# The first chunks of the first feed-forward layer: both token blocks multiplied before their norm factor is known

## The chip, the cores and the metric

The kernel runs on one core of one Trainium2 chip. The metric is the device time of one execution in microseconds (us), and lower is better. The median of three runs of the kernel before is 754.53 us (754.26 to 755.93).

## What is computed

The reference is one decoder layer in float32 over 256 tokens of width 1024: a half feed-forward layer, a mixing layer with two branches (a state-space branch and differential attention), and a second half feed-forward layer, each between two RMS norms. Only the start matters here, the first feed-forward layer (`x @ w` is a matrix product, `g` a gain per channel):

```python
def rmsnorm(x, g):
    y = x * lax.rsqrt(jnp.mean(x * x, axis=-1, keepdims=True) + EPS)
    return y * g

def swiglu(x, w_gate, w_up, w_down):          # 1024 -> 2816 -> 1024
    return (jax.nn.silu(x @ w_gate) * (x @ w_up)) @ w_down

h = x
h = h + 0.5 * rmsnorm(swiglu(rmsnorm(h, ffn1_pre_g), ffn1_w_gate, ffn1_w_up, ffn1_w_down), ffn1_post_g)
...
```

The norm's factor is one number per token. It can be taken out of a product: `(r * u) @ w` equals `r * (u @ w)`, if `r` is applied to the rows of the result. Both kernels use that, for one token block or for two.

## The kernel before

**Split numbers.** Every operand of the large products is split into a high part that TensorE takes exactly and a low part, the rest; a product is the sum of three: high x high, low x high, high x low. For weights, ScalarE casts the raw chunk to `whi` (L167) and VectorE subtracts to get `wlo` (L168). For activations, ScalarE makes the high part (L343) and VectorE the low part (L345) out of the transposed block in PSUM, each with the gain of the channel.

**Tiles.** The 256 tokens are two blocks of 128, b = 0 and 1. The 1024 channels are two halves, q = 0 and 1, of four k-tiles each. Weights come through three raw buffers of 1 MB; a buffer is loaded again when VectorE has subtracted its last part. The first four chunks are the first 512 columns of the gate weights (chunks 0 and 1, for the two halves of the channels) and of the up weights (chunks 2 and 3). Chunk 0 is loaded and split by single k-tiles, chunks 1 to 3 in two parts. Each chunk needs 4 k-tiles x 3 terms x 2 blocks = 24 matmuls of 128 x 512, 96 in all. From chunk 4 on, the kernel goes another way (`mm_w`, L206: weights stationary, both blocks at once; its first tiles are `pg_f` and `pup_f`).

**Order.** At the start the order on TensorE, ScalarE, VectorE and the DMA queue of SyncE (SP) is the program's own (`own_order`), until `free_order` behind the first four chunks. GpSimd (POOL) runs in program order too. SP loads x in four pieces of 256 KB (b0 q0, b0 q1, b1 q0, b1 q1; L274), and then the chunks (L147).

**The first norm.** ScalarE squares and sums block 0 (`sq_f`, L325), VectorE block 1 (L364), GpSimd makes the factors `r_f` (L330, L331). `turn` (L336) is the step from a block's half to its split, transposed form: four transposes on TensorE into `pu_f` (L340), then L343 and L345. Block 0 is turned without its factor, into `raw_u`; its factor is applied when its products are evicted (`settle`). Block 1 is scaled first by GpSimd (`un_f`, L373), and then turned into the tile `u_f` that the later chunks read. Block 0's part of `u_f` comes later: GpSimd puts the factors on a diagonal (`dr_f`, L378), TensorE multiplies it with ones (`rb_f`, L385), so that every partition has all factors, ScalarE copies that (`rbs_f`, L387), VectorE multiplies the transposed block with gain and factors (`us_f`, L392), and the result is split (L191, L192).

**The products.** `Norm.products` goes over (block, gate or up) in the order (0, gate), (1, gate), (0, up), (1, up), with two chunks each. Gate results are evicted through SiLU (`sg_f`, L245), up results multiplied in (L529, L531), and `back` (L537) transposes the result of a block for the down product.

**Warm-up.** `warm(WARM)` and `warm(FILL)` are matmuls of the identity that nobody reads: 6 ahead of the gain's transpose (`pt_cols_f`, L299), 8 ahead of the first product. Each is two passes of 128 columns.

Of the kernel before, what the change touches and what calls it, by code (L numbers as in the profile page):

```python
# [24 lines left out]
P = 128  # L25
# [12 lines left out]
AHEAD = 3  # L38
WARM = 6
FILL = 8  # L40
TAIL = 3
# [7 lines left out]
def tile_hybrid_layer(ctx: ExitStack, tc: tile.TileContext, x, ffn1_pre_g, ffn1_w_gate, ffn1_w_up,  # L49
# [33 lines left out]
    def bg(shape, name):  # L83
        return ps.tile(shape, F32, tag="bg", name=name, bufs=5)
# [65 lines left out]
    def split_steps(ahead=True):  # L150


        i = len(splits)
        load_to(i + 1)
        r, shape = raws[i], chunks[i][1]
        nj = shape[1] // 2
        his, los = [], []
        splits.append((his, los))
        for q in range(2):
            hi = k4([P, nj, shape[2]], f"whi{i}{q}", F32R)  # L160
            lo = k4([P, nj, shape[2]], f"wlo{i}{q}", F32R)
            his.append(hi)
            los.append(lo)
            n = 1 if i == 0 else nj
            for j in range(0, nj, n):
                js = slice(j, j + n)
                nc.scalar.copy(hi[:, js, :], r[:, q * nj + j:q * nj + j + n, :])  # L167
                nc.vector.tensor_sub(lo[:, js, :], r[:, q * nj + j:q * nj + j + n, :], hi[:, js, :].bitcast(F32))  # L168
                yield
        raws[i] = None  # L170
        if ahead:
            load_to(i + 1 + RAW_BUFS)
# [49 lines left out]
    def mm_nat(acc, w, act, k0, first, last, late):  # L222
# [7 lines left out]
        for i, ((a, b), j) in enumerate(terms):  # L230
            nc.tensor.matmul(acc, a(k0 + j), b(j), start=first and i == 0, stop=last and i == 11)  # L231


    act_since, act_fence = [], [None]
# [53 lines left out]

    pw = bg([P, P], "warm")

# [6 lines left out]
    cols_f = const.tile([P, KD], F32, name="cols_f")  # L297
    pt = bg([P, KD], "pt_cols_f")
    nc.tensor.transpose(pt, stage_f, ident[:KD, :KD])  # L299
# [35 lines left out]
    last_pool = [None]  # L335
    def turn(b, q, src, g, to, name):  # L336

        pu = bg([P, 4, P], f"pu_{name}{b}{q}")
        for i in range(4):
            nc.tensor.transpose(pu[:, i, :], src[:, i * P:(i + 1) * P], ident)  # L340
        hi, lo = to(q)
        for i in range(4):
            nc.scalar.activation(hi[:, i, :], pu[:, i, :], AF.Identity, scale=g(q * 4 + i))  # L343
        for i in range(4):
            nc.vector.scalar_tensor_tensor(lo[:, i, :], pu[:, i, :], g(q * 4 + i), hi[:, i, :].bitcast(F32),  # L345
                                           ALU.mult, ALU.subtract)
        return pu

# [8 lines left out]

    def rms(b, tag, eng=None):

        ss = tiny(2, f"ss_{tag}{b}")  # L360
        for q in range(2):
            src = h[:, b, halves[q]]
            if eng is nc.vector:
                nc.vector.scalar_tensor_tensor(jk([P, 512], f"sq_{tag}{b}{q}"), src, 1.0 / D, src, ALU.mult,  # L364
                                               ALU.mult, accum_out=ss[:, q:q + 1])
            else:
                sum_sq(ss[:, q:q + 1], src, 1.0, f"sq_{tag}{b}{q}")
        return rstd_of(ss, 1.0, f"r_{tag}{b}")
# [11 lines left out]

    def rescaled(pus, r, g, tag, dr):

        dr = diag(r, tag) if dr is None else dr
        rb = bg([P, P], f"rb_{tag}")
        nc.tensor.matmul(rb, ones, dr, start=True, stop=True)  # L385
        rbs = k2([P, P], f"rbs_{tag}")
        nc.scalar.copy(rbs, rb)  # L387
        out = []
        for q in range(2):
# [6 lines left out]

    def set_u(us):
        for q in range(2):
            split(*in_u(0)(q), us[q])

# [57 lines left out]
    class Norm:  # L458
# [3 lines left out]
        def __init__(self, tag, g):  # L462
            self.tag, self.g, self.pus = tag, g, []
            new_u(tag)
            self.to0 = in_u(0)
            self.dr = None
            self.left = []
# [8 lines left out]

        def unit1(self, engs=(nc.vector, nc.vector)):
            r = rms(1, self.tag)
            self.un = [unit(1, q, r, self.tag, engs[q]) for q in range(2)]

        def turn1(self, q):
            turn(1, q, self.un[q], self.g, in_u(1), self.tag)

        def products(self, ws, evict, at, turns=((0, 0), (0, 1), (1, 0), (1, 1)), late="u"):

            n = 0
            for b, i in turns:
                act = of_block(self.to0 if b == 0 else in_u(1))  # L490
                acc = pj(f"pn_{self.tag}{b}{i}")
                for c in range(2):
                    mm_nat(acc, ws[2 * i + c], act, c * 4, c == 0, c == 1, late if b == 0 else "u")
                    n += 1
                    for f in at.get(n, ()):
                        f()
                if b == 1:
                    evict(b, i, acc, None)
                else:
                    self.left.append(lambda i=i, acc=acc: evict(0, i, acc, self.r0))  # L500
            free_order()
# [11 lines left out]
        def rescale(self):  # L513
            set_u(rescaled(self.pus, self.r0, self.g, self.tag, self.dr))

    def ffn(post_v, tag, norm, ready, turned, then, at, ws=None, **kw):
        gu = []
# [22 lines left out]
        norm.products(ws or [take(1) for _ in range(4)], evict,  # L540
                      {n: [f if f else lambda: back(0) for f in fs] for n, fs in at.items()}, **kw)
        back(1)
# [36 lines left out]
    warm(FILL)  # L579
    load_to(1 + RAW_BUFS)  # L580

    def gains():
# [10 lines left out]
    def next_norm(tag, name):  # L593
# [68 lines left out]
    norm.products([take(1) for _ in range(4)], evict_v,  # L662
                  {3: [norm.turns1], 5: [norm.settle, norm.rescale]})

# [483 lines left out]
    ffn(ffn2_post_g, "f2", norm, store, lambda: None, lambda: None,  # L1148
        {3: [norm.turns1], 5: [norm.settle, norm.rescale], 7: [None]})

# [33 lines left out]
```

## Time and profile before

| what | value |
|---|---|
| median of three runs | 754.53 us (754.26 to 755.93) |
| the profiled execution | 753.31 us, of which 751.60 is the span of the core |
| TensorE busy | 742.0 us of the span |
| VectorE, ScalarE, GpSimd busy | 522.1, 437.9, 41.0 us |
| TensorE's granted clock over the span | 0.999 |
| TensorE busy in the first 35 us | 32.80 us |

PE is TensorE's matmuls, PEld its weight loads, DVE VectorE, ACT ScalarE, POOL GpSimd, and SPq the DMA issues of SyncE. A row of the timeline has the start and the duration in us, the engine, the line of the kernel, the operation, the tile written and the tiles read, the shape, the count of merged instructions, and in brackets the idle time in front and what ended it. The duration of a merged row runs from its first start to its last end. A matmul's duration is longer than its distance to the next, because they are pipelined.

### The profile page before, as it was taken

What the parts mean: (1) busy time and instruction counts of PE and PEld (TensorE: products, weight loads), DVE (VectorE), ACT (ScalarE), POOL (GpSimd) and SP (SyncE); (2) the same over time, 40 slices, a digit from 0 to 9 for tenths busy, and PEclk for the clock granted to TensorE, in tenths of its full rate; (3) what the DMA queues carried; (4) which work ended last, traced back from release to release, by engine and by line L of the source; (5) the groups of instructions that cost most, each with busy time, mean ns of one, the idle gap of its engine ahead of it and who ended that gap; (6) DMA issues with size and microseconds to landing.
All of it is one profiled execution on the core that took longest, in us unless ns stands there. A gap on an engine that the chain in (4) does not pass through costs nothing.

```text
span 751.6 us, 11066 instructions
## 1 busy us (share of the span) xinstructions
PE 742.0 (99%) x4385; PEld 643.8 (86%) x4385; DVE 522.1 (69%) x790; ACT 437.9 (58%) x731; POOL 41.0 (5%) x76
## 2 busy tenths in 40 slices
PE   8999999999999999999999999999999999999996
PEld 7888888888889999898999778788888888888885
DVE  6685667654577888868777987696684867766612
ACT  7475556643565565858867555783563756664511
POOL 7400000000200000000000000000010000000000
PEclk9999999999999999999999999999999999999999
DMA  8685666486253647565556454376371777544701
GB/s 316 158 276 162 222 224 240 181 280 223 64 168 115 203 135 242 169 200 183 161 168 202 166 192 152 129 230 246 112 232 49 225 223 224 177 176 184 275 1 56
DMA packets 94212, 137.96 MB, mean 184 GB/s; under 512 B 2684, under 2 KB 68304, under 8 KB 94160
## 3 DMA queue, kind: packets, MB, share of 16 engines
q1 hardware_dynamic: 91488, 129.51, 52.3%
q0 software_dynamic: 2368, 7.22, 3.2%
q8 instruction: 34, 0.56, 0.3%
q10 hardware_dynamic: 304, 0.53, 0.2%
q14 instruction: 18, 0.15, 0.1%
HBM read 136.17 MB, written 1.08 MB: 183 GB/s over the span
## 4 chain that ended last, share of the span: by engine, by line
PE 96%; DVE 1%; POOL 1%; DMA 1%; ACT 1%; issue 0%; SPq 0%; DVEq 0%; POOLq 0%; ACTq 0%
PE acc_f L433 16%; PE pup_f L216 9%; PE pg_f L216 9%; PE pws L231 6%; PE pgt L231 6%; PE pn_f L231 5%; PE pg_f L215 4%; PE pup_f L215 4%; PE acc_mx L433 3%; PE pn_mx L231 3%; PE pwd L231 3%; PE pxs L204 2%; PE pxs L202 2%; PE pxs L201 2%; PE pz L204 2%; PE pz L201 2%
## 5 line engine op out<-in xcount | busy, mean ns | idle before, releaser
L168 DVE TENSOR_TENSOR wlo<-raw,whi 128x1024 fp32r<-128x1024 f32 (+1 forms) x246 | 291.6, 1213 | 53.6 <-ACT whi L167 50.9
L167 ACT CAST whi<-raw 128x1024 fp32r<-128x1024 f32 (+1 forms) x246 | 247.3, 1044 | 56.7 <-PE acc_f L433 22.7
L216 PE MATMUL pg_f<-u_f,whi 128*128 128x512 f32 x288 | 101.2, 396 | 0.0
L216 PE MATMUL pup_f<-u_f,whi 128*128 128x512 f32 x288 | 101.1, 396 | 0.0
L215 PE MATMUL pg_f<-u_f,wlo 128*128 128x256 f32 x252 | 70.5, 280 | 0.0
L215 PE MATMUL pup_f<-u_f,wlo 128*128 128x256 f32 x252 | 70.3, 279 | 0.0
L216 PEld LDWEIGHTS pg_f<-u_f,whi 128*128 128x128 f32 x288 | 52.9, 188 | 9.8
L216 PEld LDWEIGHTS pup_f<-u_f,whi 128*128 128x128 f32 x288 | 52.7, 188 | 9.8
L433 PE MATMUL acc_f<-whi,gh_f 128*128 128x512 f32 x176 | 58.2, 390 | 0.0
L433 PE MATMUL acc_f<-wlo,gh_f 128*128 128x512 f32 x176 | 58.1, 389 | 0.0
L433 PE MATMUL acc_f<-whi,gl_f 128*128 128x512 f32 x176 | 58.1, 389 | 0.0
L215 PEld LDWEIGHTS pg_f<-u_f,wlo 128*128 128x128 f32 x252 | 47.5, 188 | 1.7
L215 PEld LDWEIGHTS pup_f<-u_f,wlo 128*128 128x128 f32 x252 | 47.5, 189 | 1.6
L220 DVE TENSOR_TENSOR su_f<-pup_f,su_f 128x256 f32<-128x256 f32 x36 | 15.2, 422 | 40.5 <-ACT su_f L219 40.5
L433 PEld LDWEIGHTS acc_f<-wlo,gh_f 128*128 128x128 f32 x176 | 33.0, 188 | 6.9
L433 PEld LDWEIGHTS acc_f<-whi,gl_f 128*128 128x128 f32 x176 | 33.0, 188 | 6.8
L433 PEld LDWEIGHTS acc_f<-whi,gh_f 128*128 128x128 f32 x176 | 33.0, 188 | 6.8
L231 PE MATMUL pgt<-whi,u_mx 128*128 128x512 f32 x128 | 34.8, 400 | 0.0
L201 PE MATMUL pz<-u_mx,whi 128*128 128x256 f32 x128 | 32.3, 288 | 0.0
L219 ACT COPY su_f<-pup_f 128x256 f32<-128x256 f32 x36 | 13.4, 371 | 32.2 <-PE pup_f L216 32.1
L202 PE MATMUL pz<-u_mx,whi 128*128 128x256 f32 x128 | 31.8, 284 | 0.0
L201 PE MATMUL pxs<-u_mx,whi 128*128 128x256 f32 x128 | 31.7, 285 | 0.0
(310 smaller groups left out, 1435.9 us busy)
## 6 DMA issues: line engine op xcount, KB each, us to landing
raw<-in_w_in_dram SPq DMA_DIRECT2D x40, 1024.0 KB, 5.4
raw<-in_ffn_w_down_dram SPq DMA_DIRECT2D x22, 1024.0 KB, 5.0
raw<-in_ffn_w_gate_dram SPq DMA_DIRECT2D x20, 1024.0 KB, 5.7
raw<-in_ffn_w_up_dram SPq DMA_DIRECT2D x20, 1024.0 KB, 5.5
raw<-in_ssd_w_branch_dram SPq DMA_DIRECT2D x8, 1024.0 KB, 5.1
acb<-acd POOLq DMA_DIRECT2D x8, 512.0 KB, 4.9
raw<-in_da_w_branch_dram SPq DMA_DIRECT2D x4, 1024.0 KB, 5.1
raw<-in_w_out_dram SPq DMA_DIRECT2D x4, 1024.0 KB, 5.0
```

Source lines behind the costliest of these rows:

```text
L167: nc.scalar.copy(hi[:, js, :], r[:, q * nj + j:q * nj + j + n, :])
L168: nc.vector.tensor_sub(lo[:, js, :], r[:, q * nj + j:q * nj + j + n, :], hi[:, js, :].bitcast(F32))
L201: nc.tensor.matmul(acc[m], wh(j)[:, cs], ah(k0 + j), start=first and j == ks[0], stop=False)
L202: nc.tensor.matmul(acc[m], wh(j)[:, cs], al(k0 + j), start=False, stop=False)
L204: nc.tensor.matmul(acc[m], wl(j)[:, cs], ah(k0 + j), start=False, stop=last and j == ks[-1])
L215: nc.tensor.matmul(acc[:, :T], wl(j)[:, cs], ah(j), start=False, stop=False)
L216: nc.tensor.matmul(acc, wh(j)[:, cs], ahl(j), start=j == 0, stop=j == KD - 1)
L219: nc.scalar.copy(dst[:, m, :], acc[:, T:])
L220: nc.vector.tensor_tensor(dst[:, m, :], acc[:, :T], dst[:, m, :], ALU.add)
L231: nc.tensor.matmul(acc, a(k0 + j), b(j), start=first and i == 0, stop=last and i == 11)
L433: nc.tensor.matmul(acc[b][q], x_[:, ts], w_(kt)[:, halves[q]], start=i == 0 and kt == 0 and x_ is ah and w_ is wh, stop=i == n - 1 and kt ...
```

## The change

Both blocks are now turned without their factor, and all four chunks are multiplied with these raw blocks. `mm_both` takes a chunk k-tile by k-tile and, within it, block by block; two accumulators are open at once. The transposes of the second halves stand inside chunk 0's products (behind 14 and 18 of 24 terms), the second block's `rb` inside chunk 1's (behind 16 terms). The factors come into both blocks' results at eviction, and into both parts of `u_f` by way of `rb`, `rbs`, `us` and the split, once for each block. GpSimd no longer scales block 1, and makes two diagonals.

SP loads the first halves of x (both blocks), then chunk 0, then the second halves, then the other chunks. VectorE casts the first k-tile of chunk 0 in ScalarE's place. VectorE squares block 0 and ScalarE block 1. `WARM` is 5 in place of 6, `FILL` 2 in place of 8. The second norms further on keep their way of working; their functions are only cut up differently.

```diff
-WARM = 6
-FILL = 8
+WARM = 5
+FILL = 2
...
-                nc.scalar.copy(hi[:, js, :], r[:, q * nj + j:q * nj + j + n, :])
+                copy = nc.scalar.copy if i + q + j else nc.vector.tensor_copy
+                copy(hi[:, js, :], r[:, q * nj + j:q * nj + j + n, :])
+                if not i + q + j:
+                    yield
                 nc.vector.tensor_sub(lo[:, js, :], r[:, q * nj + j:q * nj + j + n, :], hi[:, js, :].bitcast(F32))
...
+    def mm_both(accs, w, acts, k0, first, last, between={}):
+        wh, wl = w
+        his = [[(b, a, wh, j) for b in range(2) for a in acts[b]] for j in range(4)]
+        los = [[(b, acts[b][0], wl, j) for b in range(2)] for j in range(4)]
+        terms = his[0] + his[1] + los[0] + his[2] + los[1] + his[3] + los[2] + los[3]
+        for i, (b, x_, w_, j) in enumerate(terms):
+            nc.tensor.matmul(accs[b], x_(k0 + j), w_(j), start=first and j == 0 and w_ is wh and x_ is acts[b][0],
+                             stop=last and j == 3 and w_ is wl)
+            if i + 1 in between:
+                between[i + 1]()
...
-    for b in range(2):
-        for q in range(2):
+    for q in range(2):
+        for b in range(2):
             nc.sync.dma_start(h[:, b, halves[q]], xv[:, b, halves[q]])
-    load_to(RAW_BUFS)
+        load_to((1, RAW_BUFS)[q])
...
-    norm = Norm("f1", lambda j: cols_f[:, j:j + 1])
-    raw_u = [k4([P, 4, 2, P], f"raw_u{q}", F32R) for q in range(2)]
-    norm.to0 = lambda q: (raw_u[q][:, :, 0, :], raw_u[q][:, :, 1, :])
-    norm.r0 = rms(0, "f1")
-    r1 = rms(1, "f1", nc.vector)
-    norm.un = [unit(1, q, r1, "f1", nc.gpsimd) for q in range(2)]
-    norm.dr = diag(norm.r0, "f1")
-    norm.turn0(0)
-    for _ in split_steps(False):
-        pass
-    norm.turn0(1)
-    warm(FILL)
-    load_to(1 + RAW_BUFS)
...
+    def raised(b, q):
+        pus[b][q] = transposed(b, q, h[:, b, halves[q]], "f1")
+
+    def raw(b, q):
+        gained(pus[b][q], q, gain_f, *raw_to[b](q))
+
+    square(ss_f[0], 0, 0, "f1", nc.vector)
+    raised(0, 0)
+    raised(1, 0)
+    warm(FILL)
+    steps = split_steps(False)
+    next(steps)
+    raw(0, 0)
+    raw(1, 0)
+    for _ in steps:
+        pass
+    load_to(1 + RAW_BUFS)
+
+    def first_products(evict, back):
+        acts = [of_block(to) for to in raw_to]
+        acc = [[pj(f"pn_f1{b}0") for b in range(2)], None]
+        mm_both(acc[0], take(1), acts, 0, True, False, {14: lambda: raised(0, 1), 18: lambda: raised(1, 1)})
+        square(ss_f[0], 0, 1, "f1", nc.vector)
+        r = [rstd_of(ss_f[0], 1.0, "r_f10")]
+        dr = diag(r[0], "f10")
+        raw(0, 1)
+        raw(1, 1)
+        rb = bg([P, 2, P], "rb_f1")
+        rbs = []
+        w = take(1)
+        rbs.append(on_rows(rb[:, 0, :], dr, "f10"))
+        for q in range(2):
+            square(ss_f[1], 1, q, "f1")
+        r.append(rstd_of(ss_f[1], 1.0, "r_f11"))
+        us = rescaled(pus[0], rbs[0], gain_f, "f10")
+        dr = diag(r[1], "f11")
+        w2 = take(1)
+        mm_both(acc[0], w, acts, 4, False, True, {16: lambda: rbs.append(on_rows(rb[:, 1, :], dr, "f11"))})
+        set_u(0, us)
+        acc[1] = [pj("pn_f101"), bg([P, 512], "pn_f111")]
+        for b in range(2):
+            evict(b, 0, acc[0][b], r[b])
+        us = rescaled(pus[1], rbs[1], gain_f, "f11")
+        mm_both(acc[1], w2, acts, 0, True, False)
+        w = take(1)
+        set_u(1, us)
+        mm_both(acc[1], w, acts, 4, False, True)
+        split_to(5)
+        for b in range(2):
+            evict(b, 1, acc[1][b], r[b])
+        free_order()
+        back(0)
...
-    ws = [take(1) for _ in range(2)]
-    more = lambda: ws.append(take(1))
     made, ready, turned = next_norm("mx", "mx")
-    ffn(ffn1_post_g, "f1", norm, ready, turned, gains,
-        {1: [norm.turns1], 2: [more], 4: [norm.settle, more], 5: [norm.rescale], 7: [norm.settle, None]}, ws,
-        turns=((0, 0), (1, 0), (0, 1), (1, 1)), late="w")
+    ffn(ffn1_post_g, "f1", ready, turned, gains, first_products)
```

`transposed` and `gained` are the two halves of `turn`; `square` is one half of `rms`; `on_rows` is the matmul and copy that `rescaled` began with. `raw_to[b]` gives block b's raw tiles, `gain_f` the gain columns.

More of the change, by code (lines that the diff above doesn't have):

```diff
@@ L387, in rescaled @@
         nc.scalar.copy(rbs, rb)
+        return rbs
+    def rescaled(pus, rbs, g, tag):
         out = []
@@ L475, in turn0, with unit1, products @@
             self.pus.append(turn(0, q, h[:, 0, halves[q]], self.g, self.to0, self.tag))
[L477 removed]
+        def unit1(self):
             r = rms(1, self.tag)
[L479 removed]
+            self.un = [unit(1, q, r, self.tag, nc.vector) for q in range(2)]
         def turn1(self, q):
             turn(1, q, self.un[q], self.g, in_u(1), self.tag)
[L484 removed]
+        def products(self, evict, at):
+            ws = [take(1) for _ in range(4)]
             n = 0
[L489 removed]
+            for b in range(2):
                 act = of_block(self.to0 if b == 0 else in_u(1))
[L491 to L500, printed above, removed]
+                for i in range(2):
+                    acc = pj(f"pn_{self.tag}{b}{i}")
+                    for c in range(2):
+                        mm_nat(acc, ws[2 * i + c], act, c * 4, c == 0, c == 1, "u")
+                        n += 1
+                        for f in at.get(n, ()):
+                            f()
+                    if b == 1:
+                        evict(b, i, acc, None)
+                    else:
+                        self.left.append(lambda i=i, acc=acc: evict(0, i, acc, self.r0))
             free_order()
@@ L513, in rescale, with ffn @@
         def rescale(self):
-            set_u(rescaled(self.pus, self.r0, self.g, self.tag, self.dr))
-    def ffn(post_v, tag, norm, ready, turned, then, at, ws=None, **kw):
+            rbs = on_rows(bg([P, P], f"rb_{self.tag}"), diag(self.r0, self.tag), self.tag)
+            set_u(0, rescaled(self.pus, rbs, self.g, self.tag))
+    def ffn(post_v, tag, ready, turned, then, products):
         gu = []
@@ L538, in back @@
             split(gh[:, :, bs], gl[:, :, bs], pt_)
-        norm.products(ws or [take(1) for _ in range(4)], evict,
-                      {n: [f if f else lambda: back(0) for f in fs] for n, fs in at.items()}, **kw)
+        products(evict, back)
         back(1)
@@ L565, in ffn @@
         mm_n(acc, gu, done, turned)
[L568 to L579 removed]
+    new_u("f1")
@@ new lines, in tile_hybrid_layer @@
+    raw_u = [[k4([P, 4, 2, P], f"raw_u{b}{q}", F32R) for q in range(2)] for b in range(2)]
+    raw_to = [lambda q, b=b: (raw_u[b][q][:, :, 0, :], raw_u[b][q][:, :, 1, :]) for b in range(2)]
+    gain_f = lambda j: cols_f[:, j:j + 1]
+    pus = [[None] * 2 for _ in range(2)]
+    ss_f = [tiny(2, f"ss_f{b}") for b in range(2)]
+    def raised(b, q):
[3 more added lines that the diff above has]
+    square(ss_f[0], 0, 0, "f1", nc.vector)
@@ L660, in evict_v @@
             nc.scalar.activation(vt[c][:, b, :], acc, AF.Identity, scale=r)
-    norm.products([take(1) for _ in range(4)], evict_v,
-                  {3: [norm.turns1], 5: [norm.settle, norm.rescale]})
+    norm.products(evict_v, {3: [norm.turns1], 5: [norm.settle, norm.rescale]})
     wdt = k2([P, KD, H_SSD], "wdt")
```

42 lines of the change are left out of this document (23 added, 19 removed).

## The prediction

> **What bounds the kernel now.** I read the page first. TensorE is busy for 99% of the span, and the chain that ended last is TensorE for 96%:
>
> ```profile
> PE 742.0 (99%) x4385; PEld 643.8 (86%) x4385; DVE 522.1 (69%) x790; ACT 437.9 (58%) x731; POOL 41.0 (5%) x76
> ...
> PE 96%; DVE 1%; POOL 1%; DMA 1%; ACT 1%; issue 0%; SPq 0%; DVEq 0%; POOLq 0%; ACTq 0%
> ```
>
> So only what TensorE does, or waits for, is worth anything, and the diff touches the first 35 us alone. In the table by stage, TensorE is busy for 32.80 of the first 35.00 us and for all of 35 to 185 us: a time won or lost before 35 us moves everything behind it. Next, the timeline of TensorE there (start, duration, line, count, idle before):
>
> ```profile
> 4.45 0.27 PE L299 MATMUL pt_cols_f<-ident,stage_f 8*128 8x8 f32 x1
> 4.66 1.60 PE L340 MATMUL pu_f<-ident,h 128*128 128x128 f32 x8
> 6.09 1.95 PE L294 MATMUL warm<-ident 128*128 128x128 f32 x16
> 8.03 0.73 PE L231 MATMUL pn_f<-whi,raw_u 128*128 128x512 f32 x2
> 9.24 2.10 PE L231 MATMUL pn_f<-whi,raw_u 128*128 128x512 f32 x6 [0.47 <-ACT whi L167]
> 11.18 1.08 PE L231 MATMUL pn_f<-wlo,raw_u 128*128 128x512 f32 x4
> 12.09 1.40 PE L340 MATMUL pu_f<-ident,un_f 128*128 128x128 f32 x8
> 13.24 2.09 PE L231 MATMUL pn_f<-whi,raw_u 128*128 128x512 f32 x8
> ```
>
> The first product starts at 8.03, when the first weight k-tile has been cast, and "warm" fills the time before. The gaps behind 8.03 follow the k-tiles' landings (x: 3.5, 4.5, 5.3, 6.7; chunk 0: 7.3, 8.5, 9.2, 9.9), and the break inside L340 at 12.09 is a wait for GpSimd's un_f. From 12.83 on TensorE runs without a break: 96 products at 0.2265 us from start to start, the next stage (pg_f, L216) at 33.13. Work between 8.03 and 33.13: 96 x 0.2265 = 21.74, eight transposes 0.88, rb 0.22, one block's pt_f 0.44, together 23.28 of 25.10, so **1.8 us of waits** and **8.03 us of start** are all that can be won.
>
> Then GpSimd and VectorE, since the change puts new work of theirs in front of TensorE:
>
> ```profile
> 7.57 0.30 POOL L330 TENSOR_SCALAR r_f<-ss_f 128x1 f32<-128x1 f32 x1 [0.73 <-DVE sq_f L364]
> 7.96 0.56 POOL L331 TENSOR_TENSOR r_f<-r_f,nhalf 128x1 f32<-128x1 f32 x1
> ...
> 12.66 2.35 DVE L168 TENSOR_TENSOR wlo<-raw,whi 128x1024 fp32r<-128x1024 f32 x2
> 12.76 2.65 POOL L378 TENSOR_SCALAR dr_f<-ident,r_f 128x128 f32<-128x128 f32 x1
> ```
>
> dr_f (the factor on a diagonal) takes 2.65 us here, and 0.79 us in each of its two later cases. Here it was issued 0.1 us behind a VectorE subtraction and ended 0.4 us behind the second one (15.0). The page "SBUF — State Buffer" of the Trainium skill (Who interferes with whom) says that a VectorE instruction with two SBUF inputs and a GpSimd one that reads SBUF exclude each other, whoever issued first; this row agrees with it.
>
> **The change, part by part.** In program order TensorE gets the same 96 products and the same 16 transposes (eight before the first product, eight behind it, as before), and one more rb: +0.22 us. What moves is the start and the waits.
>
> *Start.* The queue of SP keeps its count and sizes up to chunk 1, but the chunk's four k-tiles come third to sixth instead of fifth to eighth, so I give them the landings 5.3, 6.7, 7.3, 8.5, and the second x halves 9.2 and 9.9; later issues wait for the same positions. "warm" loses one matmul, two passes of 0.213 us: transposes from 4.66 - 0.43 = 4.23. ScalarE's hi parts of block 0 began 1.15 us behind the first transpose and took 1.14 (5.81 to 6.95); now 5.38 to 6.52, and block 1's to 7.53 (the two squares that stood in front are gone). The cast of the first k-tile goes to VectorE, from 5.3: no row has it; by TENSOR_SCALAR 128x512 (0.50 us) or the subtraction of 128x512 (0.68) it is done by 6.0, under the hi parts, so it costs nothing; if it took over 1.2 us it would set the start. **First product at 6.57**, 1.46 earlier.
>
> *Chunk 0.* VectorE now makes eight lo parts at 0.26 (6.57 to 8.63) before the first wlo (0.68): 9.31. The eight terms in front of it in mm_both are 1.8 us of work, so TensorE waits in between and goes on at 9.36. Sixteen terms (3.62) and eight transposes (0.88) lead to 13.86. The other casts (landing 8.5 plus 0.62), the wlo's (0.60 apart, the last at 11.1) and x (9.9) are earlier than their terms.
>
> *First rb.* It stands in TensorE's queue, so all of chunk 1 queues behind it. VectorE squares x's second half at 11.03 to 11.81, GpSimd adds 0.30, 0.56, dr 0.79 and 0.1 per hand-over: 13.79. Hidden, by 0.1 us. rb ends at 14.08.
>
> *Chunk 1.* ScalarE makes hi parts behind the late transposes (the last four end at 12.5 after 18 terms), until 13.70, and only then casts whi10 (1.05): 14.80. **Wait 0.7.** Sixteen terms: 18.42.
>
> *Second rb.* ScalarE: whi11 to 15.8, rbs 0.2, two squares at 0.73: 17.43; GpSimd 0.30 + 0.56 + 0.79 + hand-overs: 19.42. **Wait 1.0**, with eight products of chunk 1 and chunks 2 and 3 queued behind it. dr would start at 18.58; VectorE's us (eight at 0.26, no second SBUF input) end at 19.2 and then come the two-input subtractions wlo20 and wlo21. dr is first by 0.6 us, so I take 0.79; its bounds are 0.29 (affine_select of 128x128, L634) and the 2.65 above.
>
> *The rest.* rb 0.22, eight terms 1.81: 21.45. Chunks 2 and 3, 48 terms: 10.87, to **32.32**. Their casts are ahead (whi30 at 23.7 for a use at 26.9; wlo31 at 27.1). The second set of us and u parts (block 1's rescale: eight at 0.26, two subtractions at 0.69, two casts at 0.62) is new on VectorE and ScalarE; VectorE was busy for only 7.30 of the 13 us from 20 to 33, and I find it done at 28.3. Without that room each 0.69 would come straight onto pg_f. GpSimd's un (4.15) is gone, and its DMAs of stage_a go out some 4 us later (19.4), land some 6 us later (26) and are read at 34. Raw buffers 4 to 6 are asked for 2 to 5 us later than before and have 5 us of slack.
>
> *Sum.* 33.13 less block 0's pt_f, which now comes later, is 32.69; after: 32.32. That is -0.37, and the wait of 0.17 in front of the second pt_f (34.08) goes, since both gate products are evicted by 33.9: **-0.54 us**. Put as a balance: start -1.46, extra rb +0.22, waits 2.7 (9.36 minus 6.57 minus 1.81, plus 0.72, plus 1.00) against 1.8 before, +0.9, and the -0.17. Where the old stall went: x and k-tiles are no longer late, VectorE's lo parts and GpSimd's dr are.
>
> The profiled execution took 753.31 (span 751.60, 1.71 around it): 752.8. The runs' median is 1.22 above it, 754.53, so **754.0**. With dr at 0.29: 753.5.
>
> **Rivals.**
>
> *A. The two late waits do not show* (dr at its low bound, hi parts or squares earlier by half a microsecond each): -0.54 - 0.72 - 1.00 = -2.3, 752.3. For it: dr and L634 treat as many elements, and the 0.79 rows run beside VectorE. Against: whi10 follows four hi parts at 0.25 and TensorE's own order. Chance 0.22.
>
> *B. dr is shut out.* If GpSimd's second chain slips by 0.6 us, or VectorE is early, dr starts inside wlo20 and ends as in the row above, 0.4 behind wlo21 (21.6): 22.0 instead of 19.42. +2.6 - 0.54 = +2.1, 756.6, slower. It decides at wlo20's start, 19.2. For it: 12.76 and 19.66 (affine_select m, 2.11 against 0.29 for the next one) show it twice. Against: both were issued inside a subtraction. Chance 0.14.
>
> *C. The clock comes late.* A pass of 128 columns takes 0.213 until 5.76 and 0.11 after it, so TensorE runs at half speed for its first 4.2 us of work. "warm" falls from 28 passes to 14, and 6.57 to 9.36 has gaps. If it stays at half speed past 6.57, a product takes 0.45 (twice 0.2265, an estimate from the transposes' ratio), the eight first terms 3.6, and TensorE goes on at 10.2 in place of 9.36: +0.8, net +0.3, 754.8, and 0.5 more for each further us of half speed; decided by the rate of the passes behind 5.8. Against: TensorE stays almost gapless from 1.59 to 6.3, past the 5.76 of the row. The page "TensorE: Matmul & The Clock Gate" of the Trainium skill (Why this matters for your kernels) asks for 4 us of continuous work for the full clock, which speaks against a shorter warm-up; the stretch above still meets it, so by that rule the sum stays. Chance 0.06.
>
> That the change does not do what it says I leave out: the instructions' order has the products in pairs over both blocks, and the DMAs in the order told.
>
> **How the numbers follow.** A measurement of this kernel tells 0.2% (1.5 us) from no change. Forecast 0.58 (754.0, by dr's bounds 753.5 to 754.0, "same" but for scatter of the runs, which were 754.26 to 755.93); A 0.22, mostly "faster"; B 0.14, "slower"; C 0.06, "same". Faster: 0.18 of A and 0.04 of the forecast's scatter, 0.22. Slower: B and 0.02 of scatter, 0.16. Same: 0.62. The range runs from A's time, 752.3, to 756.3, just short of B's: most of B (0.10) and what of A lies lower (0.08) are left out.
>
> **What would show it.** Right: first product near 6.6, wlo of k-tile 0 the last gap of chunk 0 near 9.4, gaps of 0.7 before whi10's first product and 1.0 before the second rb, pg_f near 32.3. Wrong: dr_f near 2.6 us; products 0.45 us apart (twice 0.2265) behind 6.6; k-tiles landing later than x did; or a wait in pg_f or pup_f for wlo or u, which would mean that VectorE had no room for the second rescale.

## The result, and the profile after

The kernel after takes **752.73 us** in the median of 14 runs (752.61 to 752.85), the kernel before 754.18 in the 14 runs beside them (753.29 to 755.93). The ratio is 0.9981, 95% interval 0.9972 to 0.9989: 1.45 us less. The profiled executions stand nearer together: 752.63 (span 750.93) against 753.31 (span 751.60), 0.68 us less. The runs of after lie within 0.24 us of each other, those of before within 2.64. So there are two things to explain: 0.68 us that the two profiles show, and the rest, which is that before is usually slower than its profiled execution and after is not.

The page of after, the busy time of each engine and the shares of the chain that ended last:

```profile
PE 740.6 (99%) x4373; PEld 642.2 (86%) x4373; DVE 525.0 (70%) x801; ACT 436.9 (58%) x733; POOL 33.3 (4%) x75
...
PE 96%; DVE 1%; ACT 1%; POOL 0%; issue 0%; DVEq 0%; POOLq 0%; ACTq 0%
```

TensorE still carries the chain. The 1% of DMA that before had is no longer among the shares. GpSimd's busy time fell by 7.7 us, and VectorE's rose by 2.9.

TensorE's timeline at the start of after:

```profile
6.00 0.47 PE L244 MATMUL pn_f<-whi,raw_u 128*128 128x512 f32 x1
6.81 0.73 PE L244 MATMUL pn_f<-whi,raw_u 128*128 128x512 f32 x2 [0.34 <-DVE raw_u L363]
7.84 1.43 PE L244 MATMUL pn_f<-whi,raw_u 128*128 128x512 f32 x5 [0.30 <-DVE raw_u L363]
9.21 0.73 PE L244 MATMUL pn_f<-wlo,raw_u 128*128 128x512 f32 x2
...
13.91 0.38 PE L410 MATMUL rb_f<-dr_f,ones 128*128 128x128 f32 x2
14.84 2.11 PE L244 MATMUL pn_f<-whi,raw_u 128*128 128x512 f32 x8 [0.55 <-ACT whi L168]
...
18.97 0.49 PE L410 MATMUL rb_f<-dr_f,ones 128*128 128x128 f32 x2 [0.20 <-POOL dr_f L405]
...
32.04 0.39 PE L219 MATMUL pg_f<-u_f,whi 128*128 128x512 f32 x1
```

The first product starts 2 us earlier than before (6.00, 8.03). The next ones wait for VectorE's lo parts, the first low part of the weights comes at 9.21, and from there two gaps are left: whi10 at 14.84 and the second rb at 18.97. pg_f starts at 32.04 in place of 33.13; of these 1.09 us, 0.44 is one block's pt_f, which now comes later; 0.65 remain, and the spans differ by 0.67.

VectorE and GpSimd of after:

```profile
5.42 0.43 DVE L168 CAST whi<-raw 128x512 fp32r<-128x512 f32 x1 [0.32 <-DMA raw<-in_ffn_w_gate_dram]
6.40 2.16 DVE L363 SCALAR_TENSOR_TENSOR raw_u<-pu_f,cols_f,raw_u 128x128 fp32r<-128x128 f32 x8 [0.55 <-ACT raw_u L361]
8.48 2.49 DVE L171 TENSOR_TENSOR wlo<-raw,whi 128x512 fp32r<-128x512 f32 x4
...
19.27 2.35 DVE L171 TENSOR_TENSOR wlo<-raw,whi 128x1024 fp32r<-128x1024 f32 x2
```

```profile
18.29 0.62 POOL L405 TENSOR_SCALAR dr_f<-ident,r_f 128x128 f32<-128x128 f32 x1
```

The second dr_f ends at 18.91, 0.36 us ahead of the pair of two-input subtractions at 19.27.

### The profile page after: what moved, and what is told of

Its sections match the earlier page's. It is cut to its first block, busy times and chain, and to the rows that moved or that the text cites. A ratio compares the mean times of both kernels' runs of the same rounds, so it can differ in the third digit from the quotient of the medians.

```text
span 750.9 us, 11051 instructions
## 1 busy us (share of the span) xinstructions
PE 740.6 (99%) x4373; PEld 642.2 (86%) x4373; DVE 525.0 (70%) x801; ACT 436.9 (58%) x733; POOL 33.3 (4%) x75
## 4 chain that ended last, share of the span: by engine, by line
PE 96%; DVE 1%; ACT 1%; POOL 0%; issue 0%; DVEq 0%; POOLq 0%; ACTq 0%
PE acc_f L462 16%; PE pup_f L219 9%; PE pg_f L219 9%; PE pws L234 6%; PE pgt L234 6%; PE pg_f L218 4%; PE pup_f L218 4%; PE pn_f L234 3%; PE acc_mx L462 3%; PE pn_mx L234 3%; PE pwd L234 3%; PE pn_f L244 2%; PE pxs L207 2%; PE pxs L205 2%; PE pxs L204 2%; PE pz L207 2%
## 5 line engine op out<-in xcount | busy, mean ns | idle before, releaser
L204 PE MATMUL pxs<-u_mx,whi 128*128 128x256 f32 x128 | 31.7, 285 | 0.0
L205 PE MATMUL pxs<-u_mx,whi 128*128 128x256 f32 x128 | 31.4, 283 | 0.0
```

Source lines behind the costliest of these rows:

```text
L204: nc.tensor.matmul(acc[m], wh(j)[:, cs], ah(k0 + j), start=first and j == ks[0], stop=False)
L205: nc.tensor.matmul(acc[m], wh(j)[:, cs], al(k0 + j), start=False, stop=False)
```

## The experiments

The pairs of medians below are from runs side by side. Over all of them, before has a median of 753.88 us in 100 runs (753.06 to 755.93), 1.15 above after; one more run of it, of 994.14 us, is not counted. After was not run beside the versions below: "above after" and "below after" mean its 752.73, from a session in which before stood 0.25 to 0.41 us higher than in the later ones (754.18 against 753.77 to 753.93). So a few tenths between a version and after rest on the rows of the profiles and not on the medians.

### What scatters before: the kernel before once more

> The kernel before, unchanged, for its scatter: its runs lie between 753.29 and 755.93 us, while those of the kernel after lie within 0.24 us, and the profiled execution before (753.31) is at the low end. Two theories of what scatters. Loads: the landings of x and of the first k-tiles differ from run to run by up to 2 us, and the first products (8.03 to 12 us) hang on them. A profile of a slow execution would have the k-tiles of chunk 0 landing 0.5 to 2 us later than 7.3, 8.5, 9.2 and 9.9, and pg_f later than 33.13 by the same. GpSimd: un_f (two of about 2 us, the second ended at 12.78, 0.12 us behind the start of a 1.1 us subtraction of VectorE) is sometimes shut out by the subtractions behind it and ends 1 to 2.6 us later, with landings unchanged; TensorE's transposes of un_f wait for it. Both theories: a median of 754.2, a spread of 1.5 us or more. A profile at 753.3 again tells nothing.

Measured: 753.91 us (753.19 to 754.28, 11 runs). The profiled execution took 754.28, which is 0.97 more than the one of before shown above. Its VectorE, GpSimd and TensorE:

```profile
7.83 0.69 DVE L364 SCALAR_TENSOR_TENSOR sq_f<-h 128x512 f32<-128x512 f32 x1 [1.42 <-DMA h<-in_x_dram]
```

```profile
9.68 4.15 POOL L373 TENSOR_SCALAR un_f<-h,r_f 128x512 f32<-128x512 f32 x2
```

```profile
9.10 2.69 PE L231 MATMUL pn_f<-whi,raw_u 128*128 128x512 f32 x8 [0.99 <-ACT whi L167]
...
13.89 0.66 PE L340 MATMUL pu_f<-ident,un_f 128*128 128x128 f32 x4 [0.51 <-POOL un_f L373]
...
34.19 0.62 PE L216 MATMUL pg_f<-u_f,whi 128*128 128x512 f32 x2
```

The loads theory holds in this execution. The square of x's last piece, which waits for the transfer, starts at 7.83 in place of 6.77; un_f starts at 9.68 in place of 8.62 and takes the same 4.15; pg_f starts at 34.19 in place of 33.13. Each is 1.06 us later, and the span is 0.97 longer. GpSimd was not shut out: its duration did not change. In before, x's fourth piece is the head of a chain (square, factor, un_f, transposes, products) without slack, so its landing goes into the time one to one. What the slower runs, up to 755.93, waited for was not seen.

### The new products with the old loads

```diff
-    for q in range(2):
-        for b in range(2):
+    for b in range(2):
+        for q in range(2):
             nc.sync.dma_start(h[:, b, halves[q]], xv[:, b, halves[q]])
-        load_to((1, RAW_BUFS)[q])
+    load_to(RAW_BUFS)
```

> The kernel after, with x and the weights loaded in the order of before (all of x, then chunk 0). The four k-tiles land fifth to eighth, at about 7.3, 8.5, 9.2 and 9.9: first product at 7.9 in place of 6.0, the products of k-tile 1 at 9.2, from there 20 products and eight transposes without a gap: chunk 0 done at 14.6 in place of 13.7, whi10 0.7 later than 14.84. Sum +0.7: 753.4, so the new load order alone would be worth 0.7 and everything else 0.0 to 0.7. Loads theory of the scatter: the spread of before, 1.5 us or more, is back, and the median lies above 754. GpSimd theory: the runs lie within 0.4 us round 753.4.

Measured: 755.68 us (754.04 to 756.91, 7 runs) beside 753.86 of before, ratio 1.0025 (1.0014 to 1.0037): slower than before, and the scatter is back, 2.9 us. TensorE in its profile (754.86 us):

```profile
8.14 3.58 PE L244 MATMUL pn_f<-whi,raw_u 128*128 128x512 f32 x8 [0.72 <-DVE whi L168]
11.56 0.63 PE L244 MATMUL pn_f<-wlo,raw_u 128*128 128x512 f32 x2
...
34.27 0.39 PE L219 MATMUL pg_f<-u_f,whi 128*128 128x512 f32 x1
```

and VectorE:

```profile
7.57 0.43 DVE L168 CAST whi<-raw 128x512 fp32r<-128x512 f32 x1 [2.46 <-DMA raw<-in_ffn_w_gate_dram]
7.91 2.15 DVE L363 SCALAR_TENSOR_TENSOR raw_u<-pu_f,cols_f,raw_u 128x128 fp32r<-128x128 f32 x8
9.98 2.49 DVE L171 TENSOR_TENSOR wlo<-raw,whi 128x512 fp32r<-128x512 f32 x4
```

The start came where expected, 8.14 for 7.9. Two things were not expected. VectorE's cast waits for the k-tile, and the lo parts stand behind the cast: they start at 7.91, in after at 6.40, so that the first low part of the weights is done 1.50 us later than in after, at 10.66 (9.98 and 0.68 for one subtraction). And the pace: the eight products take 3.58 us, most of them 0.43 from start to start in place of 0.23, until the clock is full at 11.39. So the first product with a low part starts at 11.56, 2.35 later than in after; about 1.5 of that is VectorE's order and 0.85 the clock. pg_f is 2.23 later, and this profile lies 2.23 above that of after. The median lies 2.95 above after's; what of that scatter is landings and what is the clock was not told apart.

### The new loads with the old products

The same lines exchanged the other way, in the kernel before.

> The kernel before with the loads in the new order (first halves of x, chunk 0, second halves, the rest) and nothing else of the change: the counterpart of the run with the new products and the old loads (755.68 us). Block 0 is squared whole before its hi parts on ScalarE, and block 1 needs all of x for its factor, so both now wait for second halves that land at 9.1 and 9.4. Theory: the start hangs on which piece of x is last for the first product and for GpSimd's un_f; r of block 1 comes about 2.6 us later (11.3 in place of 8.5), un_f ends at 15.4 in place of 12.8, and the kernel takes 2.6 us more than before: 756.5. So the load order alone is a loss and only pays with the new products. Rival (landings matter little, the load order is a gain of its own): 752 to 754.

Measured: 757.47 us (757.19 to 758.54, 4 runs) beside 753.77, ratio 1.0050 (1.0036 to 1.0065): 3.7 us slower; the time is 1.0 above the expected one.

```profile
9.37 1.11 PE L340 MATMUL pu_f<-ident,h 128*128 128x128 f32 x4 [3.60 <-DMA h<-in_x_dram]
...
17.04 0.66 PE L340 MATMUL pu_f<-ident,un_f 128*128 128x128 f32 x4 [0.33 <-POOL un_f L373]
```

The second half of block 0 lands at 9.35 and everything waits for it. From profile to profile it is 4.23 more than before, and 2.6 were expected. The 1.6 between them come from GpSimd, which makes block 0's factor first, so that un_f starts at 12.76 and ends at 16.99, not at 15.4; the transposes of 17.04 wait for it. The "warm" passes behind the 3.6 us of idle still run 0.213 apart, since the clock is full only at 12.96, and the first product starts only at 13.26, so that TensorE is done with block 0 just 0.33 us ahead of that. The two parts of the change need one another: products alone +1.8 us, loads alone +3.7, both together -1.45.

### The two late waits

First both at once, by earlier transposes:

```diff
-        mm_both(acc[0], take(1), acts, 0, True, False, {14: lambda: raised(0, 1), 18: lambda: raised(1, 1)})
+        mm_both(acc[0], take(1), acts, 0, True, False, {8: lambda: raised(0, 1), 12: lambda: raised(1, 1)})
```

> The kernel after, with the transposes of the second halves behind 8 and 12 terms of chunk 0 in place of 14 and 18. They then fill the wait for the first low part of the weights (9.1 to 9.5) and end at 10.9 in place of 12.5; ScalarE's hi parts end at 12.0 and its cast whi10 at 13.1, ahead of the first rb (13.6 to 13.8): the wait of 0.55 in front of chunk 1 goes. ScalarE's squares come about 1.5 us earlier, the second dr_f is done at 17.4, 16 terms of chunk 1 end at 17.45: the wait in front of the second rb goes too. Theory of the prediction (both waits are real and hang on ScalarE's place behind the late transposes): -1.0 to -1.3 us against the kernel after, 751.4 to 751.7, pg_f at 30.9. Rival (they hang on VectorE or GpSimd, or come back as another wait): -0.3 to +0.3. Rival (dr_f, now 1.7 us nearer to the subtractions of chunk 1, is shut out by one of them): +1 to +2.6.

Measured: **751.50 us** (751.30 to 751.81, 5 runs) beside 753.86 of before, ratio 0.9970 (0.9958 to 0.9982), and 1.23 below after.

```profile
9.44 0.66 PE L355 MATMUL pu_f<-ident,h 128*128 128x128 f32 x4
...
14.21 2.07 PE L244 MATMUL pn_f<-whi,raw_u 128*128 128x512 f32 x8
...
17.93 0.38 PE L410 MATMUL rb_f<-dr_f,ones 128*128 128x128 f32 x2
...
30.90 0.39 PE L219 MATMUL pg_f<-u_f,whi 128*128 128x512 f32 x1
```

Both waits are gone: chunk 1 follows the first rb (14.06) at once, and the second rb has no bracket. pg_f starts at 30.90, the expected number. Then the second wait alone:

```diff
-        mm_both(acc[0], w, acts, 4, False, True, {16: lambda: rbs.append(on_rows(rb[:, 1, :], dr, "f11"))})
+        mm_both(acc[0], w, acts, 4, False, True, {20: lambda: rbs.append(on_rows(rb[:, 1, :], dr, "f11"))})
```

> The kernel after with the second rb behind 20 terms of chunk 1 in place of 16. In the profile of after the 16 terms end at 18.46 and rb waits for dr_f until 18.97; four more terms (0.91) lead to 19.37, behind dr_f. Theory (the wait in front of the second rb is real and nothing else is late there): -0.5 us, 752.2, pg_f at 31.5 in place of 32.04. Rival (the later rb makes VectorE's second rescale or the parts of u_f late for pg_f): no gain, 752.7 or more. The run with earlier transposes (751.50) took both late waits away at once; this one takes the second alone, and leaves about 0.7 for the first.

Measured: 752.30 us (752.23 to 752.48, 11 runs) beside 753.93, 0.43 below after. rb starts at 19.72 without a wait; pg_f at 31.75, in an execution whose wlo of k-tile 0 came at 9.38, 0.17 later than in after. So of the 1.23, 0.43 is the second wait, and 0.8 the first with the gap ahead of 9.21. By the rows of the two profiles the first is worth 0.63 (chunk 1 starts at 14.21 in place of 14.84), and at the second rb 1.04 is gained in all.

### Rival B: the diagonal made inside VectorE's subtractions

```diff
         dr = diag(r[1], "f11")
+        nc.gpsimd.tensor_scalar(dr, ident, r[1], None, ALU.mult)
```

> The kernel after, with the second block's diagonal made twice by GpSimd, the issue of one DMA (0.75 us) between the two; the output is the same. The second one starts at 19.65, inside the first of VectorE's two-input subtractions wlo20 and wlo21 (19.27 to 21.62 in the profile of after), and the second rb waits for it. Rival B's mechanism (a GpSimd operation issued inside such a pair is held until 0.4 us behind it): this dr_f takes about 2.4 us and ends at 22.0, rb at 22.0 in place of 18.97, +3.0 us, 755.7. Without it: dr_f takes 0.63 again and ends at 20.3, +1.3 us, 754.1.

Measured: 757.45 us (757.20 to 757.46, 4 runs), 4.7 above after. GpSimd, then TensorE:

```profile
18.43 0.62 POOL L405 TENSOR_SCALAR dr_f<-ident,r_f 128x128 f32<-128x128 f32 x1
...
19.81 2.34 POOL L642 TENSOR_SCALAR dr_f<-ident,r_f 128x128 f32<-128x128 f32 x1
```

```profile
22.21 0.80 PE L410 MATMUL rb_f<-dr_f,ones 128*128 128x128 f32 x2 [3.32 <-POOL dr_f L642]
22.66 2.06 PE L244 MATMUL pn_f<-whi,raw_u 128*128 128x512 f32 x4
```

The same instruction takes 0.62 us outside the pair and 2.34 inside it, and ends at 22.15, 0.39 behind the pair's end (19.41 + 2.35). So rival B's mechanism is real, and the price that the prediction gave it, 2.6, was too low. rb is 3.24 us later than in after; 0.45 of that is after's rb coming earlier than predicted. Behind the idle 3.32 us TensorE's clock is also half, from 21.65 to 25.06. The eight products behind rb take 3.04 us in place of 1.81. The Trainium skill, page "SBUF — State Buffer" (Who interferes with whom), says that a two-input VectorE instruction and a GpSimd one that reads SBUF exclude each other; these two rows agree with it. A longer case is in the run with earlier transposes. GpSimd's two affine_selects of L714 take 6.40 us there, from 23.29, and 0.64 in after; VectorE makes six operations with two SBUF inputs one behind another from 23.61 to 29.44, and the second select ends 0.25 behind them. No row of TensorE waits for it.

### The warm-up and the clock

`WARM` 1 and `FILL` 1 in place of 5 and 2:

> The kernel after with WARM 1 and FILL 1 in place of 5 and 2, so that TensorE idles between 2.0 and 3.5 us and has gaps until 6. Rival C's mechanism (full clock only behind a stretch without gaps): eight products behind 6.6 start 0.43 us apart in place of 0.23, the full clock comes at 9.5 to 13 in place of 4.9, and up to 3.4 us of work costs double what is not hidden by the wait for the first low part: +0.3 to +2.0 us, 753.0 to 754.7, with more scatter than 0.24 us. Without it: the passes and products run as in the kernel after, 752.7 within 0.2.

`WARM` 6 and `FILL` 8, as before:

> The kernel after with the warm-up of before (WARM 6, FILL 8). The transposes start 0.43 us later and 16 passes stand ahead of the first product, which then starts at 7.6 with a clock that is full by 5.7, at up to 8.8 with a later one. The transposes' delay moves the chain of hi parts, lo parts and wlo of k-tile 0 by 0.4 to 9.65, and the eight terms in front of it fit in between. Theory: +0.4 us with an early clock, up to +1.0 with a late one; 753.0 to 753.6. Rival C turned round (the shorter warm-up costs clock, the longer one gives it back): 752.7 or less.

The first k-tile cast by ScalarE, as before (`copy = nc.scalar.copy` for all):

> The kernel after with the first weight k-tile cast by ScalarE again in place of VectorE. ScalarE then casts from 5.4 to 6.0, ahead of its eight hi parts, which end 0.8 us later than in after; VectorE's lo parts and the first low part of the weights follow, 10.0 in place of 9.2. Theory (the end of chunk 0 is set by the chain hi parts, lo parts, wlo of k-tile 0): +0.6 to +0.85 us, 753.3 to 753.6. Rival (it hangs on the landings or on TensorE's own work): 752.7 within 0.2.

Measured: the short warm-up 752.61 us (752.22 to 754.69, 10 runs), the old one 753.22 (752.68 to 753.88, 10 runs), the cast on ScalarE 753.50 (753.28 to 756.05, 10 runs). TensorE with the short warm-up, in an execution of 752.49:

```profile
6.34 3.07 PE L244 MATMUL pn_f<-whi,raw_u 128*128 128x512 f32 x8 [0.30 <-DVE whi L168]
9.25 0.62 PE L244 MATMUL pn_f<-wlo,raw_u 128*128 128x512 f32 x2
```

The clock is full only at 8.51, and the first products run at half speed, about 0.43 apart. The first low part follows at 9.25 all the same, in after at 9.21. Two things make that up: the wait for the first wlo, which is a reserve for the clock, and an earlier start, since with fewer passes the transposes begin at 3.65 in place of 4.23 and the lo parts at 6.11 in place of 6.40. The median is that of after, but the slowest runs are 2 us above it; their place was not seen. The old warm-up costs 0.5, inside the expected 753.0 to 753.6: its transposes come 0.43 later, and the first product at 8.16. But the eight products did not fit in front of the first low part, as expected: that was done at 9.74 (9.06 and 0.68), and they end at 10.08. Without the VectorE cast the median is 0.77 above after's, inside the expected 0.6 to 0.85. Seven of ten runs lie at 753.28 to 753.54 and three at 755.15 to 756.05. The profile is of one of these (755.15). The k-tile landed 1 us later in it, its cast at 6.40 held up ScalarE's hi parts behind it, and TensorE had 1.48 us from its last "warm" pass to the first product and 1.16 to the second. Busy times and granted clock (the last column but two) in two stretches of it:

```profile
5.02:8.43 3.41, 1.61 (x11) 1.10 (x9) 0.43 (x4) 2.03 (x7) 0.00 (x0) 1.00 0.85 300
8.43:11.84 3.41, 3.34 (x8) 2.35 (x9) 3.41 (x11) 2.21 (x6) 0.00 (x0) 0.50 1.05 402
```

and the like stretch of after:

```profile
4.91:8.32 3.41, 2.77 (x16) 1.90 (x15) 2.54 (x11) 3.09 (x11) 0.00 (x0) 1.00 0.89 286
```

TensorE was busy for 1.61 of 3.41 us, the clock then fell to half for the next 3.41, and the products there stand 0.42 to 0.59 apart. In after the like stretch has 2.77 busy, and the clock stays. This is half speed as in rival C, but lost again and not late, in a kernel with longer gaps. The cast on VectorE is worth 0.77 us in the median, and it also keeps hi parts, and with them the clock, from hanging on the k-tile's landing.

### Two versions further

Low parts of the weights last, and the factors later:

```diff
-        terms = his[0] + his[1] + los[0] + his[2] + los[1] + his[3] + los[2] + los[3]
+        terms = his[0] + his[1] + his[2] + his[3] + los[0] + los[1] + los[2] + los[3]
...
-        mm_both(acc[0], take(1), acts, 0, True, False, {14: lambda: raised(0, 1), 18: lambda: raised(1, 1)})
+        mm_both(acc[0], take(1), acts, 0, True, False, {10: lambda: raised(0, 1), 14: lambda: raised(1, 1)})
...
+        def factors():
+            rbs.append(on_rows(rb[:, 0, :], drs[0], "f10"))
...
+        mm_both(acc[0], w, acts, 4, False, True,
+                {4: factors, 20: lambda: rbs.append(on_rows(rb[:, 1, :], drs[1], "f11"))})
```

> The kernel after with its waits taken out: in each chunk the 16 terms with the weights' high part come before the eight with the low part, the transposes of the second halves stand behind 10 and 14 terms of chunk 0, the first rb behind 4 terms of chunk 1 and the second behind 20. The wait for the first low part (until 9.2) goes, since TensorE has 3.6 us of work ahead of it, and GpSimd's and ScalarE's chains have 0.9 us more for both rb. From the rows of after and of the run with earlier transposes: chunk 0 from 6.6 to 13.5 (14.06 there), chunk 1 without a wait, pg_f at 30.2 to 30.4. Theory: 750.8 to 751.1, 0.4 to 0.7 below that run (751.50) and 1.7 to 1.9 below after. Rival (the next limit is VectorE's work as a whole, or the second halves of x landing at 9.4): no gain on 751.50.

Measured: **751.35 us** (751.28 to 751.90, 6 runs) beside 753.77, ratio 0.9969 (0.9956 to 0.9981), 0.15 below the run with earlier transposes and not the expected 0.4 to 0.7; pg_f starts at 30.85, there at 30.90.

```profile
7.99 1.88 PE L244 MATMUL pn_f<-whi,raw_u 128*128 128x512 f32 x7 [0.30 <-DVE raw_u L363]
...
13.85 1.19 PE L244 MATMUL pn_f<-whi,raw_u 128*128 128x512 f32 x4
```

TensorE has no wait behind 7.99, but it starts the fourth product only then. The expectation let 24 terms run from 6.6; 21 were left at 7.99. The wait moved from 9.2 to the front. I took VectorE's order of the lo parts for the cause and made them, and ScalarE's hi parts, k-tile by k-tile for both blocks:

> The kernel with high parts first (751.35 us), with the hi and lo parts of the first halves made in the order of their use (k-tile by k-tile, both blocks) in place of block by block, and the transposes of the second halves behind 12 and 13 terms in place of 10 and 14. In its profile the fourth product waits until 7.99 for the fifth lo part, and TensorE runs without a wait from there. Theory (that order of VectorE's is the next limit): the fourth product at 7.0, chunk 0 done at 13.0 to 13.4, whi10 ready at 13.1 to 13.4, pg_f at 30.1 to 30.4 in place of 30.85, 750.6 to 750.9. Rival (whi10, behind hi parts that wait for x landing at 9.4, or the clock, is late by as much): 751.2 to 751.5.

Measured: 753.14 us (752.64 to 755.66, 11 runs), 1.8 slower. ScalarE, then TensorE:

```profile
6.62 0.63 ACT L618 ACTIVATE raw_u<-pu_f,cols_f 128x128 fp32r<-128x128 f32 x2 [0.41 <-DVE raw_u L621]
7.41 0.63 ACT L618 ACTIVATE raw_u<-pu_f,cols_f 128x128 fp32r<-128x128 f32 x2 [0.16 <-DVE raw_u L621]
```

```profile
9.38 2.10 PE L244 MATMUL pn_f<-whi,raw_u 128*128 128x512 f32 x8 [1.74 <-ACT whi L168]
```

ScalarE now waits for VectorE before each pair, and VectorE for ScalarE, so the eight parts take until 8.82 in place of 7.55 and the casts of the k-tiles behind them start at 8.72 in place of 7.39. TensorE waits 1.74 us for the first of these casts. Neither theory had this. That the two wait for each other because both parts lie in one tile is likely and was not tried.

### GpSimd relieved, which missed its aim

In the kernel before, un_f on VectorE (`nc.vector` in place of `nc.gpsimd`), to test the other theory of the scatter:

> The kernel before with block 1 scaled by VectorE in place of GpSimd, all else as it was. VectorE's scaling stands behind the four subtractions of chunk 0, two of some 0.5 us, and delays the subtractions of chunk 1 by about 1 us, of which at most 0.5 should reach TensorE: 753.3 to 754.0 for the fastest run. GpSimd theory: the scatter goes, the runs lie within 0.5 us, median 753.3 to 754.0. Loads theory: the scatter stays, 1.5 us or more between lowest and highest, median about 754.2 to 754.7.

Measured: 756.52 us (755.90 to 757.81, 5 runs) beside 753.86. With un_f gone, GpSimd's program put its later DMA issues and masks ahead of block 1's factor, which came at 14.6 in place of 8.5, and TensorE waited 3.1 us. So it tests neither theory; for one slower execution the run of before above had answered the question.

## Why the prediction was right or wrong

**The start, 6.57.** Measured 6.00. The sum let the first product wait for all four hi parts of block 0. It needs only the first of them and the cast, which ended at 5.85; in the run with hi and lo parts in pairs the row of the first product names the cast. ScalarE's hi parts also began at 5.23 in place of 5.38, since the clock was full at 4.91. The earlier start bought nothing, because the prediction's own next step held: VectorE's lo parts (6.40 to 8.56) stand in front of the first wlo. **Chunk 0 goes on at 9.36**: 9.21. The unknown cast on VectorE took 0.43, less than the 0.50 to 0.68 that it was estimated at, and it is not free in itself: it is hidden because ScalarE need not do it (+0.77 in the median when it must).

**First rb hidden by 0.1**: hidden by 0.56; dr_f was done at 13.35, with 0.63 in place of 0.79. **Wait 0.7 for whi10, to 14.80**: 14.84. **Second rb 19.42**: 18.97. dr_f started at 18.29 (18.58 in the prediction) and took 0.62 (0.79). The last two of the 16 terms start at 18.15, 0.23 apart, so rb could have started at 18.61: the wait is 0.36 and not 1.0, the most oversized term of the sum, and the run with the later rb puts it at 0.43. **pg_f 32.32**: 32.04. **pt_f's 0.17** was worth nothing: from pg_f to the first pup_f, without 0.44 for each pt_f between them, before takes 6.03 us (33.13 to 39.60, one pt_f) and after 6.02 (32.04 to 38.94, two). The second rescale had its room: VectorE's parts of u_f were done at 28.5, predicted 28.3.

**The sum, -0.54**: -0.68 from profile to profile. That it came so near is partly luck: pg_f was 0.28 earlier than in the sum, and the 0.17 of pt_f was not there to be won. **From there to 754.0 is the step that failed.** I added the 1.22 us by which before's first median stood above its profiled execution, as if they belonged to any kernel with this start. They do not. A good part of them is the chance of three runs: over 100 runs before's median stands 0.57 above that execution. The rest belongs to before, as far as the one slower execution shows it (0.97 above, with x's fourth piece 1.06 later): before's chain hangs on that landing without slack, and after does not hang on it. After's transposes of the second halves of x start at 10.71 and 12.08, and the halves land at 9.05 and 9.71. Its lo parts wait for ScalarE and not for the k-tile, whose cast started between 5.42 and 6.23 in after and four kernels with the same start (earlier transposes, later rb, diagonal twice, high parts first), while the lo parts started at 6.40 to 6.57. At 6.23 (later rb) the slack is just used up; a later k-tile would cost time in after too. After's median is 0.10 above its profile. So the predicted 754.0 was 1.27 too high, and 1.12 of that is this term. The table of before had the hint: its profiled execution lay 0.95 below the lowest of the three runs shown, so the runs were varying by something that the trace of one execution could not show.

**The chances.** -0.19% lies just inside "same". Rival A's two waits did show, at 0.7 and 0.36. Rival B's mechanism is as described; it missed by 0.36 us, the distance from dr_f's end to wlo20, and would have cost up to 4.7 and not 2.6. Rival C did not happen in the profile of after, where the clock was full at 4.91. But the instructions up to the first product are the same in four other kernels, and there it was full at 5.55 (high parts first), 7.46 (later rb), 8.00 (diagonal twice) and 8.14 (earlier transposes), though TensorE worked almost without a gap from 1.59 to 6.6, which the prediction took for enough. So rival C's condition, half speed past 6.57, came in three of five executions. The 0.06 was too low for that, and the price of 0.8 too high. The first product with a low part starts at 9.36 (diagonal twice) and 9.38 (later rb), the prediction's own number, in place of 9.21. The 0.15 comes from the slower transposes, behind which the hi parts begin at 5.38; the slow products themselves disappear in the wait for the first low part. With the old loads and with the cast on ScalarE they do not.

## What to carry to other kernels

A sum over one profiled execution gives the difference to another profiled execution; before adding the distance from profile to median, ask what in the old kernel hangs on a transfer without slack, and whether the new one does too. Three runs are also too few for that distance: it was 1.22 by three and 0.57 by 100. When an early stage is reordered, the order of the loads and the order of the work are one change: here each alone lost 1.8 and 3.7 us, and both together won. A wait that remains may be a reserve: the gap until 9.2 hid half-speed products, and it could be used in another way too: the transposes moved into it brought 1.23 us.

## What the runs showed of the hardware that was not expected

- The clock does not only come late, it also goes. Within an execution its steps lie 3.41 us apart: full at 5.02, half at 8.43, full at 11.84 (cast on ScalarE); half from 21.65 to 25.06 behind 3.32 us of waiting (diagonal twice); half from 16.11 to 19.53 (un_f on VectorE). The first full clock came at 4.91, 5.74, 8.14 and 11.39 us (after, before, earlier transposes, old loads), in executions whose first matmul was at 1.59 in all. The Trainium skill, page "TensorE: Matmul & The Clock Gate" (What's actually happening), gives a free-running window of 3413 ns and has the clock set by how busy TensorE was of late; the distances agree. A stretch of that length with TensorE busy for 1.61 us was enough to lose the clock (cast on ScalarE), one with 2.15 (parts in pairs) or 2.77 (after) was not. At half speed, 2.73 us of work in the stretch from 4.57 to 7.98 were not enough to gain it (old loads).
- Landings of the same program differ by more than a microsecond from execution to execution: x's fourth piece released VectorE at 6.77 and at 7.83 in before, and the first k-tile of chunk 0 VectorE's cast at 5.42 to 6.23 in the five kernels with after's start.
- A GpSimd operation that reads SBUF got no turn between VectorE operations with two SBUF inputs that follow one another. One of 0.62 us took 2.34 beside a pair of them (diagonal twice), and two of 0.64 together took 6.40 beside a row of six (earlier transposes).
- A cast of 128x512 to the exact part took 0.43 us on VectorE and 0.62 on ScalarE.
